# Moving the S5 parameter products of a hybrid trunk kernel: set-up and the first weight set into the even mixer's last output blocks, the other three sets to every third pair of ConvFFN tiles, one sign change to GpSimd

## The chip, the cores and the metric

The kernel runs on one core of a Trainium2 chip. The metric is the device time of one execution, in microseconds (us); shorter is better. The core's engines are named as in the profile: PE (TensorE, matrix products), DVE (VectorE), ACT (ScalarE), POOL (GpSimd) and SP (SyncE, which issues the loads of the big weights). Each engine works through a queue of its own in order; semaphores tie the queues together.

## The reference

The reference is a trunk of two layers on an input of 512 tokens by 1024 channels, in float32. Each layer is a mixer and a gated ConvFFN, each with a pre-RMSNorm and a residual add:

```
for i in range(2):
    hn = rms_norm(x, mix_norm[i])
    m = even_mixer(hn, ...) if i % 2 == 0 else odd_mixer(hn, ...)
    x = x + m
    x = x + conv_ffn(rms_norm(x, ffn_norm[i]), w_up, dw_w, dw_b, w_down)
return rms_norm(x, final_norm)

def conv_ffn(h, w_up, dw_w, dw_b, w_down):
    a = causal_dwconv(h @ w_up, dw_w, dw_b)      # width 3
    gate, up = split(a, 2)
    return (silu(gate) * up) @ w_down            # 2816 wide
```

The even mixer joins a retention and a state space scan and maps both back by one output projection. The odd mixer joins a convolution module and an S5 layer, a scan with a complex diagonal state. Of the S5 layer only the parameters matter here: from `a_re`, `a_im`, `log_step`, B and C come powers of the complex state factor, and products of these powers with B and with C. They depend on no activation, so they can be worked out at any time before the odd mixer.

## The kernel before, in words

Activations lie with channels on the partitions, 512 tokens along the free side: x is eight tiles of 128x512. A product in float32 is made of three matmuls on halves: `wload` (L83) lets SP load a weight piece into `wraw` (4 buffers), ACT casts it to `whi` (L90, 3 buffers), and DVE subtracts to get `wlo` (L91, 3 buffers); `mm3` (L98 to L102) multiplies whi by xh, whi by xl and wlo by xh.

The even mixer (`even`, L290) ends in 20 output blocks, made by `outs` and `outp` (L570 on). Behind the last head's work, head(3), come outs(0, 0), outs(12, 0), outs(4, 0, nst), outs(4, 1) and outs(12, 1, nst), each of four blocks. A block loads a 128x512 weight piece, does 12 matmuls into `po`, and DVE adds `po` to a tile of x (L573). Those with `nst` also take the next norm along: a cast xh (L161, ACT), xl (L162, DVE), a square (L131, ACT) and a sum acc (L132, DVE).

The ConvFFN (`ffn`, L173) loops over 22 pairs of tiles. A tile is 24 matmuls into `pup` (8 pieces by 3), weights of 128x1024. DVE multiplies by the norm's factor into `ffh` (L185), ACT starts `ffa` (L187), DVE adds two taps of the convolution (L190, two SCALAR_TENSOR_TENSOR), and after the second tile come silu (ACT), a product `ffg` (L197, DVE) and the split into `acth` (ACT) and `actl` (L96, DVE). Once for each pair, `ffn` calls `next(aside)`: it takes one step of a generator whose work is to run beside the ConvFFN. At the first tile, PE spreads the norm's factor (`prow`, L147), which DVE gets by a chain of small operations (`rs_y`, L116 to L121).

The generator is `s5_prep` (L617). Its set-up, up to the first `yield`, loads the parameters, makes the powers `s5p` (128x16 to 128x64 pieces, GpSimd), the products `s5m` (128x256, GpSimd), loads `cdr`, `cdi` and `s5g` by GpSimd's DMA queue, changes the sign of `cdi` (L702, DVE, 128x512) and fills `s5z`. Then come steps:
- `weights(q)`, q = 0 to 3: six 128x512 TENSOR_TENSOR on GpSimd (`cmul`, L707 to L712: w1r, s5t, w1i) and six on DVE (L772 to L777: w2r, s5u, w2i). All read two SBUF tiles;
- `store(q)`: GpSimd issues DMAs of w2r and w2i (L784), PE transposes w1r and w1i (`pw`, L790), ACT copies them, GpSimd issues their DMAs (L792), PE multiplies into `pG` (L797, L798), and DVE adds that to `s5g` (L799);
- `rot(h)`, two of them, and `toep()`.

The step table says which call of `next` takes which step. Before, with pair i of the ConvFFN: set-up at 0, weights 0 at 3, store 0 and weights 1 at 5, store 1 and weights 2 at 7, store 2 and weights 3 at 9, the first rot at 10, store 3 at 11, the second rot at 12.

A scheduler orders each engine's instructions by the order of the calls and by what is ready, so that a step's instructions spread over the calls around it. `self.add_mark` is the instruction behind which the parameters' loads are issued; it stands at the last add of outs(0, 1) in both kernels.

Of the kernel before, what the change touches and what calls it, by code (L numbers as in the profile page):

```python
# [13 lines left out]
ALU = mybir.AluOpType  # L14
# [22 lines left out]
class Trunk:  # L37
# [249 lines left out]
        return st  # L287


    def even(self, st):  # L290
        nc = self.nc
        ins = self.ins
        C = self.c
# [276 lines left out]
        def outp(k0, c, last=None):  # L570
            p = self.pp("po")
            self.proj(p, ins["weo"][c, :, k0 * P:(k0 + 4) * P], mix[k0:k0 + 4])
            add = nc.vector.tensor_tensor(self.x[c], self.x[c], p, op=ALU.add)  # L573
            if last is not None:
                self.norm_chunk(last, c)
            return add
# [10 lines left out]
        def outs(k0, half, last=None):  # L587
            for c in range(4 * half, 4 * half + 4):
                self.add_mark = outp(k0, c, last)
# [15 lines left out]
        s5_mark = self.add_mark  # L605
        group_norm(1, grp[1], ys[1])
        head(3)
        outs(0, 0)
        outs(12, 0)
        outs(4, 0, nst)  # L610
        outs(4, 1)
        outs(12, 1, nst)
        self.add_mark = s5_mark
        return nst


    def s5_prep(self):  # L617
        nc = self.nc
# [6 lines left out]
        def sm(shape=S16):  # L625
            n_[0] += 1
            return self.s5p.tile(shape, F32, name=f"s5_{n_[0]}")
# [6 lines left out]
        with self.tc.issue_after(self.dma_mark.ins), self.tc.issue_after(self.add_mark.ins):  # L634
# [7 lines left out]
            step, x, th, k, m1, m8, s, c, si, co = [sm() for _ in range(10)]  # L642
# [56 lines left out]
            cdr, cdi = self.slot("cdr"), self.slot("cdi")  # L699
            dma(cdr, ins["s5cdr"])  # L700
            dma(cdi, ins["s5cdi"])
            nc.vector.tensor_scalar(cdi, cdi, -1.0, None, op0=ALU.mult)  # L702
            gt = self.slot("s5g")
            dma(gt, ins["s5dd"])

# [99 lines left out]
                if i:  # L805
                    dma(self.tpd[n:, :, i, :], zt[n:, :].rearrange("p (b x) -> p b x", b=8))

        for step in ((), (), (weights, 0), (), (store, 0, weights, 1), (), (store, 1, weights, 2), (), (store, 2, weights, 3),
                     (rot, 0), (store, 3), (rot, 1), ()):
            for f, q in zip(step[::2], step[1::2]):  # L810
                f(q)
            yield
# [381 lines left out]
def trunk(tc, ins, out):  # L1194
    from contextlib import ExitStack
    with ExitStack() as ctx:
        k = Trunk(ctx, tc, ins)
        st = k.load_x()
        st = k.even(st)
        st = k.ffn(0, st, "mix1", k.s5_prep())  # L1200
        st = k.odd(st)
        k.ffn(1, st, "final", out=out)

# [15 lines left out]
```

## Time and profile before

| | us |
|---|---|
| median of 3 runs | 1356.87 (1356.6 to 1356.95) |
| profiled execution, its own time | 1356.25 |
| profiled execution, span of the profile | 1354.5 |
| PE busy | 1334.4 (99%) |
| DVE busy | 916.2 (68%) |
| ACT busy | 550.7 (41%) |
| POOL busy | 158.9 (12%) |

The span runs from the first to the last instruction in the profile; 1.75 us of the execution's time lie around it. Starts are in us from the start of the span. The even mixer's last output blocks lie at about 363 to 415 us, the first ConvFFN begins there. In a row of the timeline stand the start, the duration, the engine, the line, the operation and its tiles (out<-in), shapes, and the count when several of a kind follow each other; in brackets, how long the engine was idle ahead of it and what released it. A row of the waits names engine, line, what it waited for, then the us in total, how often, and the longest.

### The profile page before, as it was taken

Reading aid. Unit: us, or ns where it says so; the run is one execution under the profiler, and the core shown is the slowest. Engines: PE = TensorE matmul, PEld = TensorE weight load, DVE = VectorE, ACT = ScalarE, POOL = GpSimd, SP = SyncE. Lnnn points to the kernel's source line nnn. Section 1 sums busy time; section 2 is a strip of 40 time slices with the busy share of each in tenths; the row PEclk is TensorE's granted clock in tenths of the full one; section 3 lists DMA queues with packets and bytes.
Section 4 is the critical chain, followed back from the end, with each engine's and each line's share of the span. In section 5 each row is a group of like instructions: output and inputs, shape, how many; then the busy total and the mean of one; then the engine's idle time right before and its main releaser. Section 6 shows DMA issues by size and latency. Waiting matters only on the chain.

```text
span 1354.5 us, 17442 instructions
## 1 busy us (share of the span) xinstructions
PE 1334.4 (99%) x6676; PEld 1088.1 (80%) x6676; DVE 916.2 (68%) x1545; ACT 550.7 (41%) x775; POOL 158.9 (12%) x283
## 2 busy tenths in 40 slices
PE   9999999999999999999999999999999999999997
PEld 8788888878888777888888888557888888888887
DVE  6887877679568999877723345585877777774233
ACT  5454545444343433444422233234644444442221
POOL 0210010000307233870000000000000000000000
PEclk9999999999999999999999999999999999999999
DMA  6532233232234343553233335231433333333321
GB/s 225 158 124 71 71 109 110 70 110 70 86 124 128 109 125 109 169 162 94 86 101 98 105 100 189 96 123 63 124 102 94 101 102 93 94 92 95 102 70 63
DMA packets 50532, 146.16 MB, mean 108 GB/s; under 512 B 6544, under 2 KB 7872, under 8 KB 50448
## 3 DMA queue, kind: packets, MB, share of 16 engines
q1 hardware_dynamic: 44288, 127.49, 30.7%
q0 software_dynamic: 5872, 17.37, 4.3%
q8 instruction: 52, 0.85, 0.3%
q14 instruction: 32, 0.26, 0.1%
q10 hardware_dynamic: 288, 0.19, 0.0%
HBM read 135.03 MB, written 9.99 MB: 107 GB/s over the span
## 4 chain that ended last, share of the span: by engine, by line
PE 86%; DVE 10%; issue 1%; ACT 1%; DMA 1%; POOL 0%; DVEq 0%; SPq 0%; POOLq 0%; ACTq 0%
PE pup L102 9%; PE pup L100 9%; PE pup L101 9%; PE pdn L100 6%; PE pdn L101 6%; PE pdn L102 6%; DVE ffa L190 3%; PE po L100 3%; PE pcv L889 3%; PE po L102 3%; PE po L101 3%; DVE wlo L91 2%; PE pxbc L101 1%; PE pxbc L100 1%; PE pxbc L102 1%
## 5 line engine op out<-in xcount | busy, mean ns | idle before, releaser
L90 ACT CAST whi<-wraw 128x1024 fp32r<-128x1024 f32 (+3 forms) x246 | 231.0, 939 | 473.6 <-PE pdn L101 135.3
L91 DVE TENSOR_TENSOR wlo<-wraw,whi 128x1024 fp32r<-128x1024 f32 (+3 forms) x246 | 267.7, 1089 | 139.1 <-ACT whi L90 139.0
L100 PE MATMUL pup<-xh,whi 128*128 128x512 f32 x704 | 274.9, 390 | 2.6 <-ACT whi L90 2.6
L102 PE MATMUL pup<-xh,wlo 128*128 128x512 f32 x704 | 274.5, 390 | 2.9 <-DVE wlo L91 2.9
L101 PE MATMUL pup<-xl,whi 128*128 128x512 f32 x704 | 274.0, 389 | 0.0
L102 PEld LDWEIGHTS pup<-xh,wlo 128*128 128x128 f32 x704 | 132.1, 188 | 32.1 <-DVE wlo L91 4.8
L100 PEld LDWEIGHTS pup<-xh,whi 128*128 128x128 f32 x704 | 132.2, 188 | 30.5 <-ACT whi L90 3.5
L190 DVE SCALAR_TENSOR_TENSOR ffa<-ffh,c,ffa 128x511 f32<-128x511 f32 (+1 forms) x176 | 154.3, 878 | 2.9
L101 PEld LDWEIGHTS pup<-xl,whi 128*128 128x128 f32 x704 | 132.2, 188 | 27.2
L100 PE MATMUL pdn<-acth,whi 128*128 128x512 f32 (+1 forms) x374 | 140.9, 377 | 0.0
L101 PE MATMUL pdn<-actl,whi 128*128 128x512 f32 (+1 forms) x374 | 140.8, 377 | 0.0
L102 PE MATMUL pdn<-acth,wlo 128*128 128x512 f32 (+1 forms) x374 | 140.8, 377 | 0.0
L185 DVE TENSOR_TENSOR ffh<-pup,R 128x512 f32<-128x512 f32 x88 | 60.4, 686 | 57.7 <-PE pup L102 57.6
L232 POOL TENSOR_SCALAR x<-x,c 128x512 f32<-128x512 f32 (+1 forms) x9 | 9.1, 1014 | 735.3 <-ACT acc L128 635.8
L187 ACT ACTIVATE ffa<-ffh,c 128x512 f32<-128x512 f32 x88 | 71.8, 816 | 48.0 <-DVE ffh L185 44.9
L102 PEld LDWEIGHTS pdn<-acth,wlo 128*128 128x128 f32 x374 | 70.4, 188 | 13.0
L100 PEld LDWEIGHTS pdn<-acth,whi 128*128 128x128 f32 x374 | 70.4, 188 | 12.9
L101 PEld LDWEIGHTS pdn<-actl,whi 128*128 128x128 f32 x374 | 70.4, 188 | 12.7
L100 PE MATMUL po<-mh,whi 128*128 128x512 f32 x192 | 75.4, 394 | 0.7 <-ACT mh L95 0.7
L101 PE MATMUL po<-ml,whi 128*128 128x512 f32 x192 | 75.5, 393 | 0.0
L102 PE MATMUL po<-mh,wlo 128*128 128x512 f32 x192 | 75.5, 393 | 0.0
L95 ACT CAST acth<-ffg 128x512 fp32r<-128x512 f32 x44 | 27.3, 621 | 114.5 <-DVE ffg L197 109.9
(418 smaller groups left out, 2220.4 us busy)
## 6 DMA issues: line engine op xcount, KB each, us to landing
wraw<-in_wup_dram SPq DMA_DIRECT2D x88, 512.0 KB, 3.7
wraw<-in_wdn_dram SPq DMA_DIRECT2D x32, 512.0 KB, 3.5
wraw<-in_weo_dram SPq DMA_DIRECT2D x32, 256.0 KB, 3.0
wraw<-in_wxbc_dram SPq DMA_DIRECT2D x12, 512.0 KB, 3.7
wraw<-in_wdn_dram SPq DMA_DIRECT2D x16, 384.0 KB, 3.1
wraw<-in_wz_dram SPq DMA_DIRECT2D x8, 512.0 KB, 3.7
wraw<-in_wg_dram SPq DMA_DIRECT2D x8, 512.0 KB, 3.6
ar<-acd POOLq DMA_DIRECT2D x16, 256.0 KB, 3.9
```

Of the source, the lines that this page charges most:

```text
L90: nc.scalar.copy(hi[:, :n], raw[:, :n])
L91: (eng or nc.vector).tensor_tensor(lo[:, :n], raw[:, :n], hi[:, :n].bitcast(F32), op=ALU.subtract)
L95: self.nc.scalar.copy(hi, src)
L100: mm(out, lhsT=w[0], rhs=x[0], start=start, stop=False)
L101: mm(out, lhsT=w[0], rhs=x[1], start=False, stop=False)
L102: self.mark = mm(out, lhsT=w[1], rhs=x[0], start=False, stop=stop)
L185: nc.vector.tensor_tensor(h, p, st["R"], op=ALU.mult)
L187: nc.scalar.activation(a, h, AF.Identity, scale=dw[:, j, 2:3], bias=db[:, j:j + 1])
L190: nc.vector.scalar_tensor_tensor(a[:, s:], h[:, :T - s], dw[:, j, tap:tap + 1], a[:, s:], op0=ALU.mult, op1=ALU.add)
L232: self.nc.gpsimd.tensor_scalar(self.x[c][:, ts], self.x[c][:, ts], st["g"][:, c:c + 1], 1.0, op0=ALU.mult, op1=ALU.mult)
L889: self.mark = mm(p[64 * g:64 * g + 64, s:], lhsT=w, rhs=cin[i][g][:, :T - s], start=j == 0, stop=j == 15)
```

## The change

The generator is made before the even mixer, and `even` takes two steps of it itself: the set-up between outs(0, 0) and outs(12, 0), weights 0 between outs(12, 0) and outs(4, 0). The steps in the ConvFFN are, by pair: store 0 at 1, weights 1 at 2, store 1 at 4, weights 2 at 5, store 2 at 7, weights 3 at 8, store 3 at 10, the two rots at 11 and 12, toep at 14. The sign change of `cdi` moves from DVE to GpSimd. Lines from L702 on are two higher after the change.

```
@@ even
-    def even(self, st):
+    def even(self, st, prep):
...
         head(3)
         outs(0, 0)
+        self.add_mark = s5_mark
+        next(prep)
         outs(12, 0)
+        next(prep)
         outs(4, 0, nst)
         outs(4, 1)
         outs(12, 1, nst)
-        self.add_mark = s5_mark
         return nst
@@ s5_prep
-            nc.vector.tensor_scalar(cdi, cdi, -1.0, None, op0=ALU.mult)
+            nc.gpsimd.tensor_scalar(cdi, cdi, -1.0, 1.0, op0=ALU.mult, op1=ALU.mult)
...
-        for step in ((), (), (weights, 0), (), (store, 0, weights, 1), (), (store, 1, weights, 2), (), (store, 2, weights, 3),
-                     (rot, 0), (store, 3), (rot, 1), ()):
+        for step in ((weights, 0), (), (store, 0), (weights, 1), (), (store, 1), (weights, 2), (), (store, 2),
+                     (weights, 3), (), (store, 3), (rot, 0), (rot, 1), ()):
@@ the kernel
-        st = k.even(st)
-        st = k.ffn(0, st, "mix1", k.s5_prep())
+        prep = k.s5_prep()
+        st = k.even(st, prep)
+        st = k.ffn(0, st, "mix1", prep)
```

How instructions stand on the engines that the prediction speaks of: DVE in the last output blocks, before the change, where x_87 to x_90 are the first four tiles of x, from the add of outs(0, 0) to x_89 on:

```order
L573 TENSOR_TENSOR x_89<-x_89,po 128x512
L96 TENSOR_TENSOR ml<-gs,mh 128x512
L91 TENSOR_TENSOR wlo<-wraw,whi 128x512
L573 TENSOR_TENSOR x_90<-x_90,po 128x512
L91 TENSOR_TENSOR wlo<-wraw,whi 128x512
L573 TENSOR_TENSOR x_87<-x_87,po 128x512
L91 TENSOR_TENSOR wlo<-wraw,whi 128x512
L573 TENSOR_TENSOR x_88<-x_88,po 128x512
L91 TENSOR_TENSOR wlo<-wraw,whi 128x512
L573 TENSOR_TENSOR x_89<-x_89,po 128x512
L91 TENSOR_TENSOR wlo<-wraw,whi 128x512
L573 TENSOR_TENSOR x_90<-x_90,po 128x512
```

DVE at the same place after the change, from the end of the set-up (L699 ends it; the twelve small operations L683 to L698 stand ahead of this, between the wlo and the adds of outs(0, 0)):

```order
L573 TENSOR_TENSOR x_88<-x_88,po 128x512
L91 TENSOR_TENSOR wlo<-wraw,whi 128x512
L774 TENSOR_TENSOR w2r<-s5p,s5m 128x512
L573 TENSOR_TENSOR x_89<-x_89,po 128x512
L775 TENSOR_TENSOR s5u<-s5p,s5m 128x512
L777 TENSOR_TENSOR w2i<-s5p,s5m 128x512
L776 TENSOR_TENSOR w2r<-w2r,s5u 128x512
L91 TENSOR_TENSOR wlo<-wraw,whi 128x512
L573 TENSOR_TENSOR x_90<-x_90,po 128x512
L778 TENSOR_TENSOR s5u<-s5p,s5m 128x512
L91 TENSOR_TENSOR wlo<-wraw,whi 128x512
L779 TENSOR_TENSOR w2i<-w2i,s5u 128x512
```

The six products of weights 0 now stand among the adds and the wlo of outs(12, 0); between one add (x_89) and the wlo that follows it there are three of them.

POOL after the change, from the end of the set-up's products through the first weight set; every one of these stands ahead of the ConvFFN now:

```order
L711 TENSOR_TENSOR s5m<-s5m 128x256
L732 MEMSET s5z 128x512
L713 TENSOR_TENSOR s5m<-s_20_3559,s5m 128x256
L704 TENSOR_SCALAR cdi<-cdi 128x512
L714 TENSOR_TENSOR s5m<-s5m 128x256
L709 TENSOR_TENSOR w1r<-s5p,s5m 128x512
L710 TENSOR_TENSOR s5t<-s5p,s5m 128x512
L712 TENSOR_TENSOR w1i<-s5p,s5m 128x512
L711 TENSOR_TENSOR w1r<-w1r,s5t 128x512
L808 DMA tpd<-s5z 128x1x64
L713 TENSOR_TENSOR s5t<-s5p,s5m 128x512
L808 DMA tpd<-s5z 256x1x64
```

The sign change of cdi has come in between the last products of the set-up, and the first weight set follows without a DMA ahead of it; before, seven DMA issues of tpd stood ahead of that set's first four operations.

## The prediction

> **What bounds the kernel now.** I read the busy times by window first, then PE's waits, then the timelines of VectorE (DVE), PE and GpSimd (POOL) around those waits.
>
> Columns: window and its length, then busy us with instructions in brackets for PE, PEld, DVE, ACT, POOL, then the granted clock.
> ```profile
> 360.00:380.00 20.00, 20.00 (x92) 16.57 (x92) 11.21 (x18) 6.84 (x12) 0.00 (x0) 1.00 0.27 91
> ...
> 460.00:480.00 20.00, 18.63 (x87) 14.93 (x86) 19.52 (x18) 6.11 (x9) 8.60 (x8) 1.00 0.41 119
> 480.00:500.00 20.00, 18.38 (x90) 15.22 (x89) 18.66 (x19) 7.05 (x10) 11.04 (x12) 1.00 0.38 115
> ```
> PE is busy all of 360 to 380, in the even mixer's output blocks, where DVE has room. From 460 PE has gaps, and there DVE is full (19.52 of 20). So PE bounds the kernel, except where DVE starves it. PE's waits between 400 and 600 us say for what:
> ```profile
> PE pup L102 <- DVE wlo L91: 2.9, 3, 1.4
> PE pup L100 <- ACT whi L90: 2.6, 2, 1.6
> PE prow L147 <- DVE rs_y L121: 0.8, 1, 0.8
> ```
> All six are waits for split weights or for the norm at the head of the ConvFFN. What DVE does just before one of them:
> ```profile
> 481.13 0.68 DVE L185 TENSOR_TENSOR ffh<-pup,R 128x512 f32<-128x512 f32 x1
> 489.73 6.69 DVE L190 SCALAR_TENSOR_TENSOR ffa<-ffh,c,ffa 128x511 f32<-128x511 f32 x2
> 496.53 1.59 DVE L197 TENSOR_TENSOR ffg<-ffg,ffa 128x512 f32<-128x512 f32 x1
> 499.41 0.68 DVE L185 TENSOR_TENSOR ffh<-pup,R 128x512 f32<-128x512 f32 x1
> 501.14 1.53 DVE L190 SCALAR_TENSOR_TENSOR ffa<-ffh,c,ffa 128x511 f32<-128x511 f32 x2
> 507.96 0.68 DVE L185 TENSOR_TENSOR ffh<-pup,R 128x512 f32<-128x512 f32 x1
> ```
> and GpSimd's six products of a weight set at that time (I call the set G, and DVE's own six V):
> ```profile
> 490.06 1.07 POOL L707 TENSOR_TENSOR w1r<-s5p,s5m 128x512 f32<-128x512 f32 x1
> ...
> 493.12 1.28 POOL L709 TENSOR_TENSOR w1r<-w1r,s5t 128x512 f32<-128x512 f32 x1
> 494.48 1.40 POOL L711 TENSOR_TENSOR s5t<-s5p,s5m 128x512 f32<-128x512 f32 x1
> 495.95 1.61 POOL L712 TENSOR_TENSOR w1i<-w1i,s5t 128x512 f32<-128x512 f32 x1
> ```
> A pair of taps that takes 1.53 at 501.14 takes 6.69 beside G. DVE's operations with two SBUF inputs stand still while GpSimd runs G: the pair gets through only where G has a hole, between its fourth and fifth and its fifth and sixth operation. The Trainium skill, SBUF — State Buffer, Who interferes with whom, has this as a lock held for a whole instruction, taken by whoever starts first. The rows agree on the lock, but not on the first comer: the tap at 489.73 began 0.33 ahead of G and still lost.
>
> **The change, part by part.**
>
> *ConvFFN, a set every third pair of tiles instead of every second.* DVE's pair with a set takes 499.41 − 481.13 = 18.28, one without 507.96 − 499.41 = 8.55. PE's side, around a wait:
> ```profile
> 499.77 0.50 PE L100 MATMUL pup<-xh,whi 128*128 128x512 f32 x1 [1.62 <-ACT whi L90]
> 500.10 0.40 PE L101 MATMUL pup<-xl,whi 128*128 128x512 f32 x1
> 501.28 0.50 PE L102 MATMUL pup<-xh,wlo 128*128 128x512 f32 x1 [0.78 <-DVE wlo L91]
> 501.62 0.39 PE L100 MATMUL pup<-xh,whi 128*128 128x512 f32 x1
> 501.85 0.40 PE L101 MATMUL pup<-xl,whi 128*128 128x512 f32 x1
> ...
> 533.25 0.60 PE L790 MATMUL pw<-c,w1r 128*128 128x128 f32 x4
> ...
> 535.83 0.48 PE L100 MATMUL pup<-xh,whi 128*128 128x512 f32 x1
> ```
> Matmuls follow each other by about 0.227, so a pair (2 × 24) is 10.9, and the transposes of a stored set (533.25 to 535.83) are 2.58. Before: two pairs of DVE are 26.8, of PE 21.8 + 2.6 = 24.4; DVE loses about 2.4 for each further set. After: three pairs of DVE are 35.4, of PE 32.7 + 2.6 = 35.3: even. Within one set DVE falls 18.28 − 10.9 = 7.4 behind, and with three wlo buffers it is two tiles, 10.9, ahead. So the waits nearly go. What they cost: their listed 6.3, and with each wait 0.16 (the matmul before it is listed 0.39 long, against a step of 0.227) and 0.10 (the step behind it is 0.33): 6.3 + 6 × 0.26 = 7.9. I leave 0.3 for each of the three sets left in the ConvFFN, since the balance is even and the order of wlo within a set may shift, bounds 0 and 1: −7.9 + 0.9 = **−7.0** (−7.9 to −4.9). PE's transposes and products of a stored set are as many as before, in front of other tiles.
>
> The prow wait (0.8) is in this sum: it comes from the chain of the rsqrt, in which DVE and GpSimd met:
> ```profile
> 416.71 1.21 DVE L91 TENSOR_TENSOR wlo<-wraw,whi 128x1024 fp32r<-128x1024 f32 x1
> 417.84 0.58 DVE L121 SCALAR_TENSOR_TENSOR rs_y<-rs_b,rs_y 128x4 f32<-128x4 f32 x1
> ...
> 416.72 1.68 POOL L708 TENSOR_TENSOR s5m<-s,s5m 128x256 f32<-128x256 f32 x1
> ```
> The set-up's share of that leaves the place.
>
> *Set-up and weight set 0 between the output blocks.* PE's count there is unchanged; the question is DVE's queue, in which the split weights (wlo) stand behind V. DVE there, before:
> ```profile
> 364.87 0.68 DVE L91 TENSOR_TENSOR wlo<-wraw,whi 128x512 fp32r<-128x512 f32 x1
> ...
> 371.38 0.69 DVE L573 TENSOR_TENSOR x<-x,po 128x512 f32<-128x512 f32 x1 [1.43 <-PE po L102]
> 371.98 0.69 DVE L91 TENSOR_TENSOR wlo<-wraw,whi 128x512 fp32r<-128x512 f32 x1
> 374.10 0.69 DVE L573 TENSOR_TENSOR x<-x,po 128x512 f32<-128x512 f32 x1 [1.43 <-PE po L102]
> 374.70 0.69 DVE L91 TENSOR_TENSOR wlo<-wraw,whi 128x512 fp32r<-128x512 f32 x1
> ```
> A block is 2.72 and DVE idles 1.43 of it. By busy time alone there is room: V is 6 × 0.6 = 3.6, spread over three blocks. But the lead is two blocks: the wlo written at 374.70 is for the block that starts two blocks later, so PE wants it at 374.1 + 5.4 + two matmuls, 379.8. And GpSimd comes at the same time. Its set-up before, in the ConvFFN:
> ```profile
> 413.59 0.22 POOL L707 TENSOR_TENSOR s5p<-s5p 128x16 f32<-128x16 f32 x1 [57.46 <-DVE s5p L682]
> ...
> 419.85 0.35 POOL L712 TENSOR_TENSOR s5p<-s5p 128x64 f32<-128x64 f32 x1
> 420.34 0.58 POOL L700 DMA_DIRECT2D cdr<-in_s5cdr_dram  x1
> 420.90 0.54 POOL L701 DMA_DIRECT2D cdi<-in_s5cdi_dram  x1
> 421.43 0.54 POOL L704 DMA_DIRECT2D s5g<-in_s5dd_dram  x1
> 421.98 0.64 POOL L707 TENSOR_TENSOR s5m<-s,s5m 128x256 f32<-128x256 f32 x1
> ...
> 423.82 0.54 POOL L730 MEMSET s5z<- 128x512 f32 x1
> 424.31 0.81 POOL L711 TENSOR_TENSOR s5m<-s,s5m 128x256 f32<-128x256 f32 x1
> ```
> After, in the order shown above the prediction: DVE's first set-up products stand right behind the wlo of 364.87, so GpSimd starts at about 365.8. Its powers took 413.59 to 420.2, 6.6, in which the 1.68 of s5m lay that now comes behind them: about 5.0, and up to 0.8 for meeting two wlo: done at 371 or so. One s5m (0.6) and three DMA issues (1.7): 373.3. Three products of 128x256 (421.98 to 423.82, 1.8): 375.1. Memset (0.5): 375.6. Then nothing that opens a hole: s5m 0.75, the sign change of cdi, s5m 0.8, and four operations of G (490.06 to 494.40, 4.4). The sign change on GpSimd is not in this trace; a like one is:
> ```profile
> L232 POOL TENSOR_SCALAR x<-x,c 128x512 f32<-128x512 f32 (+1 forms) x9 | 9.1, 1014 | 735.3 <-ACT acc L128 635.8
> ```
> so 1.0. GpSimd holds on for 0.75 + 1.0 + 0.8 + 4.4 = 7.0, to 382.6; then a DMA issue (0.6), the fifth operation, an issue, and the sixth, to about 386.8. On DVE, behind the x add of 374.10, stand three products of V and then that wlo, all with two SBUF inputs. The first product waits for the three s5m and passes in the memset; the other two and the wlo meet the 7.0. If one passes in each hole, they pass at 382.6, 384.6 and 386.8, and the wlo is there at 387.5: PE stands 7.7. If all three pass in the first hole, it is there at 384.5: 4.7. I take the middle, **+6.2**, with bounds of 0 (everything passes in time) and 7.7. Before, the same work met DVE where the lead was 10.9; here the lead is half of that.
>
> This trace has no standstill of PE of such a length (its longest wait in the ConvFFN is 1.6), and its clock is 1.00 in every window, so that what a restart costs after it is open: from 0 to one block at half the clock, 12 × 0.227 = 2.7 more. No row stands nearer to one end, and I take the middle, **+1.3**. The Trainium skill, TensorE: Matmul & The Clock Gate, the part on the HAM clock gate, has the clock fall to half after an idle window of about 3.4 us and come back after a busy one as long; by that, half of 3.4 is lost, an estimate of 1.7 in place of 1.3.
>
> DVE's own sign change (0.68, and a wait of 1.8 for cdi's DMA ahead of it, inside DVE's lag at 424) goes; it was covered by the same lead, and is in the −7.0. SP's loads keep their order. GpSimd's DMA issues are before anything that needs them: cdi's took 3.04 from issue to landing, and is wanted 2.9 after it: 0.2 at most.
>
> Sum: 1356.25 − 7.0 + 6.2 + 1.3 = 1356.75 for the profiled execution (span 1354.5 and 1.75 around it), which lies 0.6 under the median of 1356.87. So 1357.4.
>
> **The rivals.**
>
> *The wlo just slips past.* If GpSimd is 2 to 3 us later than I worked out, or DVE keeps its turn through the three products and the wlo (done by 377.5), the next wlo, wanted at 382.5, is the late one: behind the same 7.0 from 377.5 it is there at 385.2 to 386.7, PE stands 2.7 to 4.2, and the time is 1352.6 to 1354.1. For: the margins at 373 to 376 are tenths. Against: in the row of 416.72 GpSimd got in behind the one wlo, although DVE had more to do.
>
> *No standstill.* GpSimd opens holes around the sign change and between the s5m, as at the memset, and DVE slips through each time: 0 to 1, 1349.9 to 1350.9. For: DVE has 1.43 idle in each block. Against: the four first operations of G left no hole at 490.
>
> *The whole standstill and a slow restart.* If every product passes alone (7.7) and the first block behind it runs at half the clock (2.7), it is 1356.9 − 7.0 + 10.4 = 1360.3, slower. The point from which this decides is a standstill and restart of 9.7 together. For: at 489.73 the pair passed hole by hole, as the 7.7 supposes. Against: no row shows the clock fall, and one early hole in GpSimd's 7.0 us takes 2 us or more off. The same side is reached if the sets in the ConvFFN keep the upper bound of 1 each instead of 0.3: 1357.4 + 2.1 = 1359.5.
>
> **How the numbers follow.** A measurement of this kernel can tell about 0.2%, 2.7 us, from no change, so the bounds are 1354.2 and 1359.6. A standstill of 4.7 to 7.7 with a restart short of the worst, 1354.6 to 1359.5: 0.39, no change. Slipped past: 0.20, with up to 2.7 for a restart on top up to 1356.8; three quarters faster, one quarter no change. No standstill: 0.19, faster. The worst standstill and restart: 0.15, waits left over in the ConvFFN: 0.07, slower both. So faster 0.34, same 0.44, slower 0.22. The likeliest case has 1357.4, its own range is 1354.6 to 1359.5. The range reaches from no standstill, 1350.0, to the slow restart, 1360.3.
>
> **What would show it.** Right: PE's waits for pup gone or under 0.5 each; one wait of PE po L102 for wlo of 5 to 8 us near 380, behind DVE's products (L775 to L777) at several us each beside G; GpSimd's first G at 378 to 387. Wrong: no wait of po over 1 us there; or G beginning much later; or waits of over 1 us left at pup in each set; or, for the slow restart, matmuls 0.45 apart after the standstill.

## The result, and the profile after

| | before | after |
|---|---|---|
| median, same chip | 1356.73 (1356.31 to 1356.95, 4 runs) | 1349.34 (1348.39 to 1349.73, 4 runs) |
| profiled execution, its own time | 1356.25 | 1349.29 |
| span of the profile | 1354.5 | 1347.5 |

The ratio after to before is 0.9941 [0.9928, 0.9954]: faster, by 7.4 us in the medians and by 7.0 in the spans. The measured time lies 0.7 below the low end of the range. The forecast said no change; what came is nearest the rival without a standstill (1349.9 to 1350.9), 0.6 below its own range.

PE's waits after the change, from 360 to 600 us (total us, times, longest):

```profile
PE po L102 <- DVE wlo L91: 0.6, 1, 0.6
```

The six waits of before (6.3 us for pup and prow) are gone, and one of 0.6 has come in the output blocks. Busy times by window, with the columns as in the prediction:

```profile
360.00:380.00 20.00, 20.00 (x93) 16.50 (x92) 16.45 (x34) 6.92 (x13) 12.80 (x30) 1.00 0.34 111
380.00:400.00 20.00, 19.38 (x85) 15.41 (x84) 19.36 (x25) 8.55 (x16) 15.49 (x17) 1.00 0.64 163
...
480.00:500.00 20.00, 20.00 (x90) 16.57 (x89) 18.31 (x25) 8.93 (x12) 4.22 (x6) 1.00 0.47 131
```

The two upper rows are the output blocks: DVE goes from 11.21 to 16.45 of 20 in the first and is full in the second (19.36), GpSimd is at 12.80 and 15.49, and still PE is busy for 20.00 and 19.38. The last row is the ConvFFN, where PE had 18.38 and now has 20.00, as in every window from 400 to 580. The place where the forecast saw PE stand, on DVE:

```profile
374.93 1.58 DVE L775 TENSOR_TENSOR s5u<-s5p,s5m 128x512 f32<-128x512 f32 x1
376.44 1.11 DVE L777 TENSOR_TENSOR w2i<-s5p,s5m 128x512 f32<-128x512 f32 x1
377.48 0.68 DVE L776 TENSOR_TENSOR w2r<-w2r,s5u 128x512 f32<-128x512 f32 x1
378.08 1.10 DVE L91 TENSOR_TENSOR wlo<-wraw,whi 128x512 fp32r<-128x512 f32 x1
...
379.70 0.68 DVE L778 TENSOR_TENSOR s5u<-s5p,s5m 128x512 f32<-128x512 f32 x1
380.30 1.55 DVE L91 TENSOR_TENSOR wlo<-wraw,whi 128x512 fp32r<-128x512 f32 x1
```

and on GpSimd at the same time:

```profile
376.39 0.62 POOL L713 TENSOR_TENSOR s5m<-s,s5m 128x256 f32<-128x256 f32 x1
377.75 0.89 POOL L704 TENSOR_SCALAR cdi<-cdi 128x512 f32<-128x512 f32 x1 [0.75 <-DMA cdi<-in_s5cdi_dram]
378.62 1.16 POOL L714 TENSOR_TENSOR s5m<-s5m 128x256 f32<-128x256 f32 x1
379.75 1.55 POOL L709 TENSOR_TENSOR w1r<-s5p,s5m 128x512 f32<-128x512 f32 x1
381.27 1.50 POOL L710 TENSOR_TENSOR s5t<-s5p,s5m 128x512 f32<-128x512 f32 x1
...
384.21 1.74 POOL L711 TENSOR_TENSOR w1r<-w1r,s5t 128x512 f32<-128x512 f32 x1
```

The disputed wlo, wanted at 379.8, is there at 379.2: L775 got through at GpSimd's memset (375.90), and from 377.01 to 377.75 GpSimd waits for cdi's DMA (0.75), in which L777 gets through; L776 and the wlo follow before G begins. G began at 379.75, 1.5 later than worked out (382.6 − 4.4 = 378.2), as the rival with the slipped wlo supposes. But the next wlo, which that rival lets stand to 385 or later, went at 380.30 beside the first product of G and was done at 381.85. DVE and GpSimd take turns here: each product of G follows the one before by 1.5 us instead of 1.02, and in each there is one operation of DVE. In the trace of before, by contrast, four products of G, 1.02 apart, ran through while a pair of taps stood; only its fifth and sixth (494.48 and 495.95), behind the hole that the prediction names, are 1.47 apart, each with an operation of DVE beside it. So two questions were open: when DVE stands beside GpSimd and when it takes turns; and which part of the change brought the gain in the ConvFFN.

### The profile page after: what moved, and what is told of

Same layout as the page of the kernel before. It is cut to its first block, busy times and chain, and to the rows that moved or that the text cites. A ratio compares the mean times of both kernels' runs of the same rounds, so it can differ in the third digit from the quotient of the medians.

```text
span 1347.5 us, 17450 instructions
## 1 busy us (share of the span) xinstructions
PE 1333.4 (99%) x6676; PEld 1088.8 (81%) x6676; DVE 908.1 (67%) x1544; ACT 551.2 (41%) x775; POOL 160.9 (12%) x284
## 4 chain that ended last, share of the span: by engine, by line
PE 94%; DVE 3%; ACT 1%; issue 1%; DMA 0%; SPq 0%; DVEq 0%; ACTq 0%
PE pup L100 12%; PE pup L102 12%; PE pup L101 12%; PE pdn L101 6%; PE pdn L100 6%; PE pdn L102 6%; PE pcv L891 3%; PE po L102 3%; PE po L100 3%; PE po L101 3%; PE pxbc L101 1%; PE pxbc L100 1%; PE pxbc L102 1%; PE pqk L100 1%; PE pg L101 1%; PE pg L100 1%
## 5 line engine op out<-in xcount | busy, mean ns | idle before, releaser
L190 DVE SCALAR_TENSOR_TENSOR ffa<-ffh,c,ffa 128x511 f32<-128x511 f32 (+1 forms) x176 | 134.6, 766 | 3.0
```

Of the source, the lines that this page charges most:

```text
L190: nc.vector.scalar_tensor_tensor(a[:, s:], h[:, :T - s], dw[:, j, tap:tap + 1], a[:, s:], op0=ALU.mult, op1=ALU.add)
```

## The experiments

All differences below are of medians, against before on the same chip (1356.9 to 1357.1 there). In the expectations, *balance* is the forecast's reason for the ConvFFN (three pairs of DVE against three of PE), and its rival, *lag*, says that what DVE loses to the set-up and the first sets at the ConvFFN's head is what is missing later. For the standstill, *start* says that who starts first holds out, *kind* that taps stand and products or subtractions pass.

### Where the gain in the ConvFFN comes from

**Before, with sets at every third pair** (store and weights joined as before, nothing moved to the even mixer):

```
-for step in ((), (), (weights, 0), (), (store, 0, weights, 1), (), (store, 1, weights, 2), (), (store, 2, weights, 3),
-             (rot, 0), (store, 3), (rot, 1), ()):
+for step in ((), (), (weights, 0), (), (), (store, 0, weights, 1), (), (), (store, 1, weights, 2), (), (),
+             (store, 2, weights, 3), (rot, 0), (), (store, 3), (rot, 1), ()):
```

> The kernel before with a set every third pair, store and next weights in the same call as before (weights 0 at pair 3, then 6, 9, 12, store 3 at 15); set-up stays in the ConvFFN. Theory of the spacing (DVE's time for a set fits into three pairs): PE's waits for pup fall from 5.5 to under 0.5, prow's 0.8 stays, 1350 to 1351.5. Theory of the start (the taps caught by G cost the waits, 5 us in each set): the taps' pair still takes 6.7 in each set and half or more of the waits stay, 1353 to 1356. Theory of the lag (the set-up and G at the ConvFFN's first pairs use up the lead): the first set keeps its wait, 1353 to 1355.

Measured: 1352.95 us, ratio 0.9968 [0.9955, 0.9981], 4.0 less. PE's waits from 360 to 640:

```profile
PE pup L102 <- DVE wlo L91: 2.4, 3, 1.4
PE prow L147 <- DVE rs_y L121: 0.8, 1, 0.8
```

The spacing alone takes half of the waits away, not all. A tap still stands for over 5 us beside each of the four sets.

**Before, with store and weights apart**, at every second pair:

```
+for step in ((), (), (weights, 0), (store, 0), (weights, 1), (store, 1), (weights, 2), (store, 2), (weights, 3),
+             (store, 3), (rot, 0), (rot, 1), ()):
```

> The kernel before with a set every second pair as before, but store and weights in calls of their own, one pair apart (weights 0 at pair 3, store 0 at 4, weights 1 at 5 and so on). Theory of the spacing: no better than before, 1355 to 1357, waits for pup 4 us or more. Theory of the start: G now begins behind another DMA issue, the pair of taps takes about 2.2 in place of 6.7, waits for pup under 2, 1350 to 1352.5. Theory of the lag: 1353 to 1356.

Measured: 1355.4, ratio 0.9988 [0.9978, 0.9997], 1.6 less. Four waits for pup remain (4.6 us) and that for prow (0.8). Separating store and weights is worth little, and it did not bring the turns that *start* expected: a tap stands 5.12 us beside each of the three later sets.

**After, with the rhythm of before**: set-up and set 0 in the output blocks, the other sets at every second pair.

```
+for step in ((weights, 0), (), (), (), (), (), (store, 0, weights, 1), (), (store, 1, weights, 2), (),
+             (store, 2, weights, 3), (rot, 0), (store, 3), (rot, 1), ()):
```

> The changed kernel (set-up and weights 0 between the output blocks, sign change on GpSimd) with the rhythm of before in the ConvFFN: store 0 and weights 1 at pair 5, then at 7 and 9, store 3 at 11. Theory of the spacing: prow's 0.8 and the first set's wait go, the rest stays, 1353.5 to 1356. Theory of the start: the pairs of taps take 6.7, waits as before but for prow, 1354 to 1356. Theory of the lag: the lead of 10.9 is whole at the first set, and with DVE losing 2.5 a set the waits stay under 1, 1349 to 1350.5.

Measured: 1350.89, ratio 0.9955 [0.9938, 0.9971], 6.1 less. PE's waits from 360 to 640, one row:

```profile
PE po L102 <- DVE wlo L91: 2.2, 2, 1.6
```

No wait for pup is left, although two pairs of taps still stand for 6.6 and 6.7 us beside G, and sets come at every second pair. That is what *lag* says: with its lead whole at the ConvFFN's head, DVE carries them. DVE's own waits agree: from 430 to 540 us it waits for pup 7.0 us here and 3.7 in after, and not at all before the change or in the kernel with the spacing alone. These moves take work out of the ConvFFN's head and restore the lead in one step, and the runs do not part the two. What is left is in the output blocks: 0.6 as in after, and 1.6 because GpSimd took up weights 1 at once, far ahead of its step (so that only two of GpSimd's sets meet the ConvFFN here), as GpSimd's timeline shows:

```profile
391.20 3.64 POOL L808 DMA_DIRECT2D tpd<-s5z  x5
394.55 1.39 POOL L709 TENSOR_TENSOR w1r<-s5p,s5m 128x512 f32<-128x512 f32 x1
```

**After, with sets at every second pair, store and weights apart**:

```
+for step in ((weights, 0), (), (store, 0), (weights, 1), (store, 1), (weights, 2), (store, 2), (weights, 3),
+             (store, 3), (rot, 0), (rot, 1), ()):
```

> The changed kernel with a set every second pair of tiles (store 0 at pair 1, weights 1 at 2, store 1 at 3, weights 2 at 4, and so on), everything else as changed. Theory of the lag: DVE begins the ConvFFN with the whole lead of 10.9 and loses at most 2.4 in each of three sets, so nothing waits: 1349 to 1350. Theory of the spacing: waits of pup of 2 to 5 us in all come back: 1351.5 to 1354.5.

Measured: 1349.88, ratio 0.9949 [0.9932, 0.9965], 7.2 less, with one wait of 1.0 for pup and one of 0.6 for po. Three of GpSimd's sets lie in the ConvFFN here, and a tap still stands for 5.1 us beside two of them. Once the set-up is moved, the spacing is worth some tenths; this ratio's interval holds after's ratio.

**After, with the set-up alone moved** (the second `next(prep)` in `even` left out, so that set 0 comes with the first step of the ConvFFN):

```
-        next(prep)
         outs(4, 0, nst)
```

> The changed kernel without the second step between the output blocks: set-up there, weights 0 and all later steps one pair later in the ConvFFN (weights 0 at pair 0, store 0 at 2, weights 1 at 3). Theory of the lag (what pays is that the set-up and the first G leave the ConvFFN's first pairs): GpSimd's G of weights 0 still follows its set-up at about 385, only DVE's six products go to the ConvFFN, where the lead takes them: 1349 to 1350, no wait of pup over 0.5. Theory of the spacing: the same, since three pairs stay. If the second step's place is worth something of its own: 1351 or more, with waits of pup at the first two sets.

Measured: 1351.42, ratio 0.9958 [0.9943, 0.9973], 5.7 less; no wait for pup, two for po (2.9 us); neither expectation holds whole, since the time is over 1351 without the waits for pup. GpSimd ran ahead here too, and this shows the standstill in the output blocks themselves. GpSimd:

```profile
379.70 4.24 POOL L807 DMA_DIRECT2D tpd<-s5z  x6
383.56 1.47 POOL L708 TENSOR_TENSOR w1r<-s5p,s5m 128x512 f32<-128x512 f32 x1
...
386.62 1.67 POOL L710 TENSOR_TENSOR w1r<-w1r,s5t 128x512 f32<-128x512 f32 x1
```

and DVE:

```profile
380.90 7.95 DVE L162 SCALAR_TENSOR_TENSOR xl<-x,c,xh 128x512 fp32r<-128x512 f32 x1 [0.19 <-ACT xh L161]
388.77 0.67 DVE L573 TENSOR_TENSOR x<-x,po 128x512 f32<-128x512 f32 x1
```

Three steps from 383.56 to 386.62 are 1.02 each, and xl stands until the fourth product has ended (388.3). It began 2.66 ahead of the first product, while GpSimd was still issuing DMAs, and did not get through beside these either. So the place is not what decides. What differs from after is what stands ahead of G on GpSimd: DMA issues here, a wait and products there.

The waits account for all six kernels to within 0.7 us, each wait at its listed length and 0.26 for its edges, as the prediction prices them:

| kernel | waits from 360 to 640 | with edges | less than before's 7.9 | span against 1354.5 |
|---|---|---|---|---|
| after | 0.6 (1) | 0.9 | 7.0 | −7.0 |
| apart, moved | 1.6 (2) | 2.1 | 5.8 | −6.5 |
| even moves only | 2.2 (2) | 2.7 | 5.2 | −5.5 |
| set-up only | 2.9 (2) | 3.4 | 4.5 | −5.0 |
| three pairs, nothing moved | 3.2 (4) | 4.2 | 3.7 | −3.4 |
| two pairs apart, nothing moved | 5.4 (5) | 6.7 | 1.2 | −0.9 |

### The sign change, and the standstill that was forecast

**After, with the sign change back on DVE**:

```
-            nc.gpsimd.tensor_scalar(cdi, cdi, -1.0, 1.0, op0=ALU.mult, op1=ALU.mult)
+            nc.vector.tensor_scalar(cdi, cdi, -1.0, None, op0=ALU.mult)
```

> The changed kernel with the sign change of cdi on DVE, as before. DVE's queue then holds it ahead of a wlo, and it waits for cdi's DMA (landed at 377.7 in the changed kernel), with two adds, two wlo and weights 0 behind it. If the move to GpSimd is worth nothing: 1349 to 1349.7. If the wait inside DVE's queue counts: PE waits 1 to 4 us for wlo in the output blocks, 1350.5 to 1353.5.

Measured: 1355.75, ratio 0.9991 [0.9981, 1.0]: only 1.35 less than before, against 7.4, so this one instruction is worth about 6 us here, more than was expected of it. PE's only wait from 360 to 640 in this kernel:

```profile
PE po L102 <- DVE wlo L91: 5.9, 1, 5.9
```

DVE ahead of it:

```profile
376.45 2.49 DVE L704 TENSOR_SCALAR cdi<-cdi 128x512 f32<-128x512 f32 x1 [4.42 <-DMA cdi<-in_s5cdi_dram]
378.86 4.17 DVE L91 TENSOR_TENSOR wlo<-wraw,whi 128x512 fp32r<-128x512 f32 x1
```

GpSimd:

```profile
376.35 0.61 POOL L713 TENSOR_TENSOR s5m<-s,s5m 128x256 f32<-128x256 f32 x1
376.93 1.04 POOL L709 TENSOR_TENSOR w1r<-s5p,s5m 128x512 f32<-128x512 f32 x1
377.94 0.71 POOL L714 TENSOR_TENSOR s5m<-s5m 128x256 f32<-128x256 f32 x1
378.61 0.57 POOL L808 DMA_DIRECT2D tpd<-s5z  x1
379.19 1.07 POOL L710 TENSOR_TENSOR s5t<-s5p,s5m 128x512 f32<-128x512 f32 x1
...
381.21 1.26 POOL L711 TENSOR_TENSOR w1r<-w1r,s5t 128x512 f32<-128x512 f32 x1
```

and PE:

```profile
383.08 0.79 PE L102 MATMUL po<-mh,wlo 128*128 128x512 f32 x1 [5.89 <-DVE wlo L91]
383.68 0.63 PE L100 MATMUL po<-mh,whi 128*128 128x512 f32 x1
...
387.94 0.63 PE L101 MATMUL po<-ml,whi 128*128 128x512 f32 x1
388.37 0.47 PE L102 MATMUL po<-mh,wlo 128*128 128x512 f32 x1
```

DVE's queue waits 4.42 for cdi's DMA with the wlo behind it. GpSimd waits for nothing now: its rows from 376.35 on follow each other without a gap, and beside them the sign change takes 2.49 (0.68 before, at 423.97), and the wlo stands through the next three products until 382.5. An undisturbed wlo (0.68) would have been there 3.5 sooner, so about 2.4 of the 5.9 is the queue with the sign change, and 3.5 the wlo's own standstill. The twelve matmuls from 383.08 to 388.37 take 5.29 instead of 2.72: the restart costs another 2.6.

### When DVE stands beside GpSimd

These kernels hold only G's six products beside taps, subtractions or products of DVE, at start times shifted against each other.

**Behind memsets, and the price of a restart.** 24 starts of G behind a GpSimd memset, with four taps or four additions beside it; then 60 matmuls, six times, behind waits of growing length.

```
nc.gpsimd.memset(s[:, :256], 0.0)
...  # six products on GpSimd
for sh in (1, 2, 1, 2):
    nc.vector.scalar_tensor_tensor(a[:, sh:], h[:, :T - sh], c[:, sh:sh + 1], a[:, sh:], ...)
```

> This kernel leaves out the whole trunk and writes zeros: 24 times it starts GpSimd's set of six products (G) and, after a DVE memset of growing width, four DVE operations with two SBUF inputs (12 times SCALAR_TENSOR_TENSOR, 12 times TENSOR_TENSOR); then PE runs seven stretches of 60 matmuls, held off in between by DVE work of growing length. Theory of the start (what decides is whether a DVE operation is in flight when G's first product begins): where a DVE operation begins 0.1 to 0.6 us ahead of G, it takes 4 to 5.5 us, to the gap behind G's fourth product; where it begins behind G's start, it passes between two products (about 1.5 us each) and G's products stretch from 1.05 to about 1.5. Theory of the kind (SCALAR_TENSOR_TENSOR loses to G, TENSOR_TENSOR takes turns): the first twelve all stand 3 to 5 us whatever the phase, the others about 1.5 each. For the restart: either the matmuls are 0.227 apart behind every standstill (no cost), or behind those over some length they are about 0.45 apart for a few us.

Measured: no standstill in any of the 24. (G reads what the memset wrote and begins 0.08 behind it.) Four operations took 5.7 to 6.8 us, one between each two products, for both kinds and every start. GpSimd in the first of them, the taps beside it from 11.03 to 16.78:

```profile
12.86 1.70 POOL L38 TENSOR_TENSOR g<-s5p,s5m 128x512 f32<-128x512 f32 x1
14.53 1.70 POOL L39 TENSOR_TENSOR g<-s5p,s5m 128x512 f32<-128x512 f32 x1
```

Neither *start* nor *kind* explains the row at 489.73. PE's blocks of 60 matmuls behind a wait, three of the six; without a restart the row would be 59 steps of 0.227 and the last matmul's listed 0.39, 13.8:

```profile
272.75 16.53 PE L68 MATMUL po<-xr,w 128*128 128x512 f32 x60 [3.57 <-DVE w L65]
...
319.49 15.43 PE L68 MATMUL po<-xr,w 128*128 128x512 f32 x60 [8.61 <-DVE w L65]
...
377.97 16.81 PE L68 MATMUL po<-xr,w 128*128 128x512 f32 x60 [16.17 <-DVE w L65]
```

After standstills of 3.6 us and more, a restart costs 1.6 to 3.0. By window (PE, PEld, DVE, POOL busy, granted clock) around the first:

```profile
272.00:274.00 2.00, 1.25 (x3) 1.05 (x4) 0.66 (x2) 0.00 (x0) 0.50 0.00 0
...
278.00:280.00 2.00, 2.00 (x9) 1.63 (x8) 0.00 (x0) 0.00 (x0) 0.91 0.03 8
```

The clock is at half from 272.75 to about 278.4, more than 5 us, and 1.00 from 280 on.

**Memset or DMA issue ahead of G.** 44 starts, behind two memsets or two DMA issues of GpSimd, G with plain operands or spread ones (broadcast views, as the kernel has them).

```
if first == "dma": nc.gpsimd.dma_start(w, s)
else:              nc.gpsimd.memset(s, 0.0)
```

> This kernel leaves out the whole trunk and writes zeros: 44 times it starts two GpSimd memsets or two GpSimd DMA issues and behind them G, while DVE does a memset of growing width, a subtraction (like a wlo), the two taps (SCALAR_TENSOR_TENSOR) and a product; in half of them G reads plain 128x512 tiles, in the other half the spread views of the trunk's G (each value repeated along a dimension). Theory of the DMA issue (a tap in flight when G starts behind a DMA issue stands until G's first gap): only behind DMA issues, and only where a tap begins 0.1 to 0.5 us ahead of G, one tap takes 4 to 5.4 us and G's first four products keep a step of about 1.03 (1.22 for plain ones). Theory of the views: the same, but only with the spread views, behind memsets too. If neither, every operation of DVE passes between two products in all 44, about 1.5 us each.

Measured: behind memsets, for which G again waits 0.08, 0 of 22 stand; behind DMA issues, in 21 of 22 an operation of DVE stands for 4.8 to 6.0 us through G's first four products, the subtraction as well as a tap, with plain and with spread operands. The operands and the kind of operation do not matter; what stands ahead of G on GpSimd does.

**A memset between DMA issue and G, in the kernel.** Before, with a memset of 128x256 of w1r ahead of each set:

```
+            eng.memset(w1r[:, :256], 0.0)
             cmul(v(w1r), v(w1i), pw(qr), pw(qi), mt(bbr), mt(bbi), v(t1))
```

> The kernel before, with one GpSimd memset of 128x256 (into w1r, which G's first product writes over) between the DMA issues and G in each weight set; the order on every other engine stays. Theory of the DMA issue (a DVE operation in flight when G starts right behind a DMA issue stands until G's gap; behind a memset they take turns): the pair of taps beside G takes 2.2 to 3.5 in place of 6.7, PE's waits for pup fall from 5.5 to under 2.5, 1351 to 1354. If the memset does not separate them: pairs of 6.7 and 1356.5 to 1358.

Measured: 1354.75, ratio 0.9985 [0.9975, 0.9995]; the pairs of taps beside three of the sets still take 5.65, 6.95 and 6.95. Beside the set at 429.62 no operation takes more than 2.79, though GpSimd went from the DMA issues through the memset into it without a gap.

The same with a memset of 128x8:

> The same with a memset of 128x8 only (about 0.1 us). If it is the kind of the operation right ahead of G that counts, as the one above: 1351 to 1354. If it is the time since the DMA issue that counts: as before, pairs of 6.7, 1356.3 to 1357.5.

Measured: 1355.84, ratio 0.9992 [0.9983, 1.0001], with pairs of 6.75 to 6.91. A memset between does not end the standstill as a rule. In these two kernels the product that now came first does not need what the memset wrote, so GpSimd went on without a gap. Why the first of them gained 2 us stays open; PE's listed waits are 5.6 us in five there, against 6.3 in six.

**A memset that G waits for.** DMA issues, then memsets of 0 to 2048 columns into what G reads:

```
nc.gpsimd.dma_start(wd, sd); nc.gpsimd.dma_start(we, sd)
for k in range(0, mems, T): nc.gpsimd.memset(s[:, :min(mems, T)], 0.0)
```

> This kernel leaves out the whole trunk and writes zeros: GpSimd issues two DMAs, does memsets of 0, 8, 512, 1024 and 2048 columns in all, and then G; a sixth group has a memset of 512 and no DMA issue. DVE starts its two taps and a product at seven distances from G's start in each group. Theory of a state left by the DMA issue (it lasts until GpSimd leaves a gap, whatever it does in between): an operation of DVE stands 4 to 5.4 us in all five groups with DMA issues, wherever one is in flight at G's start, and none in the sixth. Theory of a time since the issue: the standing is gone from a certain length of memset on (512 or 1024 columns, 0.5 to 1 us). Theory of the neighbour: it is gone with any memset, which the two kernels with a memset ahead of G already speak against.

Measured: with no memset 7 of 7 pairs stand (5.5 to 6.9 us); with any memset, from 8 columns on, 0 of 28 (1.5 to 2.4); without DMA issues 0 of 7. The memset that G waits for leaves a gap of 0.09 us on GpSimd.

**Gap or memset.** Four groups of seven starts: A, DMA issues and a memset that G does not need; B, DMA issues and a gap of 1.08 us; C, memsets without DMA issue or gap; D, DMA issues and a memset of 8 columns that G waits for.

```
if grp == "A": nc.gpsimd.memset(u[:, :256], 0.0)   # not read by G
if grp == "D": nc.gpsimd.memset(s[:, :8], 0.0)     # read by G
```

> This kernel leaves out the whole trunk and writes zeros: four groups of seven starts of G, with DVE's two taps and a product at growing distance. A: two DMA issues, a memset of 256 columns that G doesn't need, then G without a gap. B: two DMA issues, then G kept waiting for DVE by about 1.5 us. C: no DMA issue, two memsets, G without a gap. D: two DMA issues, a memset of 8 columns into what G reads, so that G's first product waits for it. Theory of the gap (behind a DMA issue GpSimd keeps DVE out until it has left a gap, however short): in A an operation of DVE stands 4 to 5.4 us in most starts, in B, C and D none, about 1.5 us each. If the gap alone counted, without any DMA issue: C stands as A does. If the DMA issue left a state over a time of 1 to 2 us: A stands, and B and D in part.

Measured: in A 6 of 7 pairs stand, in B, C and D none. One start of A and one of D, on GpSimd, and below them the pairs of taps that go with them, on DVE:

```profile
28.47 0.54 POOL L46 DMA_DIRECT2D w2d<-s5t  x1
29.00 0.33 POOL L48 MEMSET s5u<- 128x256 f32 x1
29.28 1.07 POOL L61 TENSOR_TENSOR g<-s5p,s5m 128x512 f32<-128x512 f32 x1
...
240.25 0.54 POOL L46 DMA_DIRECT2D w2d<-s5t  x1
240.78 0.12 POOL L52 MEMSET s5p<- 128x8 f32 x1
240.99 1.55 POOL L61 TENSOR_TENSOR g<-s5p,s5m 128x512 f32<-128x512 f32 x1
```

```profile
28.31 5.82 DVE L68 SCALAR_TENSOR_TENSOR ffa<-ffh,c,ffa 128x511 f32<-128x511 f32 x2
...
240.09 1.53 DVE L68 SCALAR_TENSOR_TENSOR ffa<-ffh,c,ffa 128x511 f32<-128x511 f32 x2
```

From 240.78 + 0.12 to 240.99 is the gap. So in these kernels it takes both: a DMA issue on GpSimd's queue, and no gap from there to G. C has no DMA issue, D has one but a gap. With both, an operation of DVE with two SBUF inputs that is under way when G begins, or begins up to 0.10 behind it, mostly stands until GpSimd pauses; the 0.08 that the profile lists between G's fourth and fifth product is enough, and from there on they take turns. B adds little: its taps began only 0.08 to 0.17 behind G's start, and in the pair of A that went through the second tap began 0.12 behind it. Two starts do not fit: in the first one of the preceding run, without a memset, the profile lists 0.10 between the DMA issue and G, and the tap stood (5.34); and beside the set at 429.62 in the kernel with the longer memset DVE took turns without a gap.

With this, the rows of after and of the kernel with the sign change on DVE can be read alike. In both GpSimd issues three DMAs in the set-up (372.4 to 374.0) and goes on without a gap, and DVE stands beside it. In after the sign change then waits 0.75 for cdi's DMA on GpSimd itself: a gap, and turns behind it through G's first four products, with no DMA issue among them. With the sign change on DVE there is no gap, and the standing goes on through G. But there a further DMA issue (378.61) also stands right ahead of the three products beside which the wlo stood; it began 0.33 ahead of the first of them. That it is the gap alone that parts these two was not tried apart from this, since the sign change also moves the order of G on GpSimd.

What in the issue does it was not found. Nor was the edge. One pair of group A (2.29 us, its first tap 0.67 ahead of G's start) went through, and one in the DMA half of the 44 starts (0.63 ahead), while taps 0.53 and 0.59 ahead stood. In the two that went through the second tap began 0.12 and 0.15 behind G's start; no operation that stood in these small kernels began later than 0.10 behind it, but one in the kernel with the short memset did (0.14). After's sets in the ConvFFN are on the lucky side of it. Such a pair on DVE:

```profile
434.10 0.69 DVE L185 TENSOR_TENSOR ffh<-pup,R 128x512 f32<-128x512 f32 x1 [1.31 <-PE pup L102]
...
436.88 2.21 DVE L190 SCALAR_TENSOR_TENSOR ffa<-ffh,c,ffa 128x511 f32<-128x511 f32 x2
```

and G on GpSimd:

```profile
436.88 0.55 POOL L794 DMA_DIRECT2D w1d<-s5u  x1 [0.60 <-ACT s5u L793]
437.45 1.10 POOL L709 TENSOR_TENSOR w1r<-s5p,s5m 128x512 f32<-128x512 f32 x1
438.52 1.50 POOL L710 TENSOR_TENSOR s5t<-s5p,s5m 128x512 f32<-128x512 f32 x1
```

G is right behind a DMA issue, the pair began 0.57 ahead of it, and takes 2.21. The sets at 472.81 and 508.16 repeat it to within a hundredth. The row of 434.10 shows DVE waiting for PE: it is ahead, which at the same time in before it was not.

## Why the prediction was wrong, point by point

**The ConvFFN, −7.0: right in size, for half of the right reason.** All six waits went, 7.9 with their edges, which is the prediction's own bound. That a wait of 0.9 came in the output blocks and makes the sum 7.0 again is chance. The reason given, that three pairs of DVE and three of PE are even, carries 4.0 by itself. The moved set-up and first set carry 6.1 with the old rhythm, since DVE then enters the ConvFFN with its lead whole. In after the pairs of taps beside the sets also take 2.21 and not the 6.69 that the balance was worked out with. The prediction had "The set-up's share of that leaves the place" for the prow wait alone, and not for the sets behind it.

**The standstill, +6.2: the step that failed.** The prediction read the pair at 489.73 as a rule: "DVE's operations with two SBUF inputs stand still while GpSimd runs G". The row is right, but G began right behind DMA issues there, without a gap:

```profile
488.76 1.28 POOL L784 DMA_DIRECT2D w2d<-w2i  x2 [1.78 <-DVE s5g L799]
```

So did the set at 464.01. In the changed kernel a gap had come between, both engines took turns, and the wait that came of the whole move is 0.6 in place of 6.2. "Then nothing that opens a hole" is the sentence that fails: the hole was among the prediction's own numbers, as the wait of the sign change for cdi's DMA, and it was priced (0.2, measured 0.75) as a delay of GpSimd, with no thought of what it does to DVE. Every product of G behind it let one operation through.

**The restart, +1.3: did not occur, and was put low.** After a standstill of 5.9 it costs 2.6, after others 1.6 to 3.0; the bound of 2.7 was somewhat too low. From the Trainium skill, TensorE: Matmul & The Clock Gate, the part on the HAM clock gate, the prediction worked out an estimate of 1.7; the runs agree that the clock falls to half (0.50), and their 1.6 to 3.0 lie about at that estimate or above it.

**The sign change, counted within the −7.0: missed by 6 us.** It was costed where it stood before, covered by the lead of the ConvFFN, and not where the set-up was to stand. There DVE's queue holds a wlo behind it for 6.9 us (4.42 + 2.49), and GpSimd has no gap ahead of G. With it on DVE the forecast's sizes come out, the wait (5.9 for 6.2), a restart and nearly the total (1355.75 for 1357.4), but only in part for its reason: 2.4 of the 5.9 are the queue behind the sign change, which the prediction did not have, and 3.5 the wlo's standstill.

**The rivals.** "No standstill" had 0.19 against 0.39 for the forecast. Its "against", that the four first operations of G left no hole at 490, was the same unexamined row. "The wlo just slips past" was right that G would come later, by 1.5, and wrong on the next wlo. The Trainium skill, SBUF — State Buffer, Who interferes with whom, lets whoever starts first hold the pair for a whole instruction; by that, DVE and GpSimd take turns, as they do at 379.75, but it does not give the standstill through four instructions behind a DMA issue, nor that a tap begun 0.53 ahead loses.

**"What would show it wrong"** named it: no wait of po over 1 us.

## What to carry to other kernels

Before a stall in one place is taken as the price of two engines meeting, look at what each queue holds just ahead of it, and whether the same stands ahead in the new place: here turns cost an operation 0.7 to 0.9 us, and behind a DMA issue of GpSimd with no gap they became a standstill of 5. Work beside a loop costs least where the follower's lead is whole, and a set-up at the loop's head takes that lead from everything behind it. An instruction that waits for a DMA is priced by what is queued behind it in the new place.

## What the runs showed of the hardware that was not expected

- Two GpSimd products of 128x512 with DVE beside them: 1.02 apart when DVE stands (1.22 with plain operands), 1.5 (1.7) with one DVE operation between when they take turns.
- Behind a DMA issue without a gap DVE's two-input operations stood in 21 of 22, 7 of 7 and 6 of 7 starts, for 5 to 7 us with the pair; with a gap of about 0.09 us behind a memset that G waits for in 0 of 35; without a DMA issue in 0 of 60, of which 7 had no gap either. One start with a gap of 0.10 and no memset stood.
- A restart of PE after 3.6 to 21 us costs 1.6 to 3.0 us at a granted clock of 0.50; after a wait of 2.37 in the kernel with the set-up alone moved, the matmuls behind the first were 0.23 apart, so nothing beyond that wait's edge.
- The sign change on DVE, a TENSOR_SCALAR with one SBUF input, stood too (2.49 for 0.68) beside GpSimd's products without a gap; no run tried that form by itself.
